# A hybrid attention and retention block in fp32: order of the Strassen sets, of their sums and of their loads

## The chip, the cores and the metric

The kernel runs on one core of a Trainium2 chip. The metric is the device time of one execution in microseconds, as the median of several runs. TensorE (PE) multiplies, VectorE (DVE), ScalarE (ACT) and GpSimd (POOL) do the rest, SyncE (SP) and ACT issue the DMA transfers. Each engine works through its own list of instructions in program order.

## The reference

A layer over 2048 latent tokens and 256 context tokens of width 1024. The input projection makes queries, keys, values and gates for two groups of heads: neighbourhood attention (NA) and retention (RET).

```python
def _mixer(h_lat, h_ctx, w_in, ...):
    na_q, na_k, na_v, na_g, r_q, r_k, r_v, r_g = _split_proj(h_lat @ w_in)   # 8 groups of 512 columns
    cna_q, cna_k, cna_v, cna_g, cr_q, cr_k, cr_v, cr_g = _split_proj(h_ctx @ w_in)
    ...
    y_na = _merge(o_na) * jax.nn.silu(na_g)
    ...
    y_ret = _head_rmsnorm(o_ret, ret_norm_g).astype(dt) * jax.nn.silu(r_g)
    y_lat = jnp.concatenate([y_na, y_ret], axis=-1) @ w_out
```

The change touches the projection of the latent tokens to NA values (columns 1024 to 1535), NA queries (0 to 511), NA gates (1536 to 2047) and RET gates (3584 to 4095).

## The kernel before

Every fp32 operand is cut into a high and a low part (hi and lo, type fp32r); a product is three matmuls: hi by hi, hi by lo, lo by hi. The normalised tokens stand in blocks of 512 tokens, each an hhi and an hlo tile of 128 x 8 x 512 (`blk[b]`); two blocks fit, the others are stored to HBM (hS) and read again. Weights come in halves of 512 KB into st tiles (`load_w`, L176 on SP; four such tiles, each free again when its cuts have read it).

After the keys and the context the program makes two rounds. Round 1 has blocks 0 and 1, round 2 blocks 3 and 2.

1. **Values** (`values`): eight units `u_v`, four with the weights of columns 1024 (two pairs of token groups for each block) and four with those of 1280. A unit is 48 matmuls (L365); ACT evicts one half (L403), VectorE the difference (L404), SP stores it (vB, L413). Between the units' matmuls `h_sums` puts sums of the blocks: two `first`, two `second`, two `third` steps on 128 x 1024 and four `fourth` steps on 128 x 512, each a chain of VectorE adds, an ACT copy (L524) and a subtraction for the low part (L525, on POOL, for one key on VectorE). After units 4 to 6 comes `w_sums` for the first set: p0 cuts a11 and a12, p1 makes four sums and cuts a22, p2 cuts s4, p3 (after unit 7) cuts s3 and s2. Each cut is an ACT copy (L579) and a POOL subtraction (L580).
2. **Six sets** (`strassen`, `w_set`), one for each group of 256 columns in the order of `SETS`: a Strassen scheme with seven products of twelve matmuls (L626). Their order is a11, a12, s4, a22, s2, s3, s1. The function `step(n)` runs after the second, fourth, sixth and seventh product; there the next set's weight sums, the next load_w and the round's other work (`hooks`) are put. Columns under 512 are q: they are scaled, split (L635 ACT, L636 DVE) and stored in 512 KB (qS). The others are gates: Silu (L640) and a store of 256 KB (gS, ggS). `defer` issues a store some ticks later.

The hooks of round 1 store blocks (spill_step), add up the gate of the residual (`wo_gate`, gacc and wraw) and, in the last set, read block 3 and then block 2 (`take`, L769). `wo_open` closes the context's pool, opens the pool gp and clears gacc (L686). Before round 2 the weights of columns 1280 are cut (L336 on ACT, L338 on POOL for the first half and on VectorE for the second). The hooks of round 2 scale the rows of w_out (`wo_mul`, L707 to L712) and store them (woS). After round 2 come the remaining projections (their evictions are at L440), the attention and the output.

Of the kernel before, what the change touches and what calls it, by code (L numbers as in the profile page):

```python
# [9 lines left out]
F32 = mybir.dt.float32  # L10
# [3 lines left out]
ALU = mybir.AluOpType  # L14
# [4 lines left out]
P = 128  # L19
# [63 lines left out]
def hybrid_kernel(ctx: ExitStack, tc: tile.TileContext, a: dict, out: bass.AP):  # L83
    nc = tc.nc
    f = lambda ap: ap[:].bitcast(F32)
# [382 lines left out]

    run_acts(-1)

    SETS = (1536, 1792, 3584, 3840, 0, 256)
    fseq = [(u_rv, 3072), (u_rk, 2560), (u_rq, 2048), (u_rv, 3328), (u_rk, 2816), (u_rq, 2304)]
    fseq += [(u_rv, 3328), (u_rv, 3072), (u_rk, 2560), (u_rq, 2048)]
    CTXU = [(2560, u_rk), (2816, u_rk), (3328, u_rv), (3072, u_rv)]
# [37 lines left out]

    def h_sums(T, A, B):
        (ah, al), (bh, bl) = ((f(x) for x in blk[b]) for b in (A, B))
        tl = {}

        def tile_(key, name, dt=F32R):
            tl[key] = hy.tile([P, 2, KH, 512], dt, name=name)

        V, G = nc.vector.tensor_tensor, nc.gpsimd.tensor_tensor  # L520

        def cut(key, ks, d):
            t = tl[key]
            nc.scalar.copy(t[:, 0, ks, :], d)  # L524
            (V if key == 3 else G)(t[:, 1, ks, :], d, f(t)[:, 0, ks, :], ALU.subtract)  # L525

        def first(c):
            if c == 0:
                tile_(0, "hhi", F32)
                tile_(3, "hlo")  # L530
            ks, kt = slice(2 * c, 2 * c + 2), slice(KH + 2 * c, KH + 2 * c + 2)
            d, e = tl[0][:, 0, ks, :], tl[0][:, 1, ks, :]
            V(d, bh[:, kt, :], bh[:, ks, :], ALU.subtract)
            G(e, bl[:, kt, :], bl[:, ks, :], ALU.subtract)
            V(d, d, e, ALU.add)
            cut(3, ks, d)

        def second(c):
            if c == 0:
                tile_(2, "hhi")  # L540
            ks = slice(2 * c, 2 * c + 2)
            d = tl[0][:, 0, ks, :]
            V(d, d, ah[:, ks, :], ALU.add)
            V(d, d, al[:, ks, :], ALU.add)
            cut(2, ks, d)

        def third(c):
            if c == 0:
                tile_(4, "hlo")
            ks, kt = slice(2 * c, 2 * c + 2), slice(KH + 2 * c, KH + 2 * c + 2)  # L550
            d = tl[0][:, 0, ks, :]
            V(d, ah[:, kt, :], d, ALU.subtract)
            V(d, d, al[:, kt, :], ALU.add)
            cut(4, ks, d)

        def fourth(k):
            if k == 0:
                tile_(1, "hhi")
                T.extend(tl[n] for n in (1, 3, 2, 4))
                tl["o"] = env["st"].tile([P, 2, 512], F32, name="o3", bufs=1)  # L560
            d = tl["o"][:, k % 2, :]
            V(d, bh[:, k, :], ah[:, k, :], ALU.subtract)
            V(d, d, bl[:, k, :], ALU.add)
            V(d, d, al[:, k, :], ALU.subtract)
            cut(1, k, d)

        return [lambda fn=fn, c=c: fn(c) for fn, n in ((first, 2), (second, 2), (third, 2), (fourth, KH)) for c in range(n)]

    def w_sums(rw):
        cut2 = lambda t: t.rearrange("p k w -> p (k w)").rearrange("p (s h k c) -> p s h k c", s=2, h=2, k=KH)  # L570
        a11, a21 = rw[0][:, :, 0:P], rw[0][:, :, P:WG]
        a12, a22 = rw[1][:, :, 0:P], rw[1][:, :, P:WG]
        W, tl = {}, {}

        def cut(key, n, s, r):
            if n not in tl:
                tl[n] = cut2(wa.tile([P, KC, WG], F32R, name=("whi", "wlo")[n % 2]))
            t = W[key] = tl[n][:, s]
            nc.scalar.copy(t[:, 0], r)  # L579
            nc.gpsimd.tensor_tensor(t[:, 1], r, f(t)[:, 0], ALU.subtract)  # L580

        V = nc.vector.tensor_tensor

        def p0():
            cut("a11", 0, 0, a11)
            cut("a12", 0, 1, a12)

        def p1():
            V(a11, a11, a21, ALU.subtract)
            V(a12, a12, a22, ALU.subtract)  # L590
            V(a12, a12, a11, ALU.add)
            V(a21, a21, a22, ALU.add)
            cut("a22", 1, 1, a22)

        def p2():
            cut("s4", 1, 0, a12)
            V(a22, a22, a11, ALU.subtract)

        def p3():
            cut("s3", 2, 1, a11)  # L600
            cut("s2", 2, 0, a22)

        def p4():
            cut("s1", 3, 0, a21)

        return W, [p0, p1, p2, p3, p4, load_w]

    def plain_next(res):
        def p1():
            res.append(w_split(wcur.pop(0), lo=1))  # L610

        return [None, p1, None, None, None, None]

    def w_set(c0, W, T, A, B, mine, ahead, hooks):
        isq = c0 < 512
        t1, t3, t2, t4 = (tuple(t[:, e] for e in range(2)) for t in T)
        b11, b21 = (tuple(x[:, e * KH:(e + 1) * KH, :] for x in blk[A]) for e in range(2))
        b22 = tuple(x[:, KH:, :] for x in blk[B])
        lay = (lambda x: x.rearrange("p (j r c) -> p j r c", r=8, j=4)) if isq else (lambda x: x)
        pv_ = (lambda x: x.rearrange("p (r j c) -> p j r c", r=8, j=4)) if isq else (lambda x: x)  # L620

        def prod(w, h):
            pm = ptile()
            for k in range(KH):
                for i, (ww, hh) in enumerate(((w[:, 0], h[0]), (w[:, 0], h[1]), (w[:, 1], h[0]))):
                    nc.tensor.matmul(pm, ww[:, k, :], hh[:, k, :], start=(k == 0 and i == 0), stop=(k == KH - 1 and i == 2))  # L626
            return pv_(pm)

        def out_tile(extra=False):
            o = env["st"].tile([P, 2, 512], F32R, name="o3", bufs=1) if extra else op.tile([P, 2, 512], F32R, name="o")  # L630
            return o, lay(f(o)[:, 1, :])

        def fin(o, ct, b):
            if isq:
                nc.scalar.activation(o[:, 0, :], f(o)[:, 1, :], AF.Copy, scale=0.125)  # L635
                nc.vector.scalar_tensor_tensor(o[:, 1, :], f(o)[:, 1, :], 0.125, f(o)[:, 0, :], ALU.mult, ALU.subtract)  # L636
                store(qS[c0 // P + ct][b], f(o))
                return
            g = f(o)[:, 1, :]
            nc.scalar.activation(g, g, AF.Silu)  # L640
            dst = gS[(c0 - 1536) // P + ct] if c0 < 2048 else ggS[(c0 - 3584) // P + ct]
            store(dst[:, b * 512:(b + 1) * 512], g)

        def step(n):
            tick()
            for fn in mine[4 + n:5 + n] + ahead[n:n + 1]:
                if fn:
                    fn()
            if hooks:
                for h in hooks.pop(0):  # L650
                    h()

        V = nc.vector.tensor_tensor
        et = wo["p"].tile([P, 2, 512], F32, name="e")
        s1, u3 = (lay(et[:, e, :]) for e in range(2))
        oa, xa = out_tile()
        nc.scalar.copy(s1, prod(W["a11"], b11))
        V(xa, prod(W["a12"], b21), s1, ALU.add)
        step(0)
        m3 = prod(W["s4"], b22)  # L660
        fin(oa, 0, A)
        m4 = prod(W["a22"], t4)
        step(1)
        ob, xb = out_tile(True)
        V(xb, prod(W["s2"], t2), s1, ALU.add)
        V(u3, prod(W["s3"], t3), xb, ALU.add)
        oc, xc = out_tile()
        V(xc, m4, u3, ALU.add)
        V(xb, m3, xb, ALU.add)
        fin(oc, 1, A)  # L670
        step(2)
        m5 = prod(W["s1"], t1)
        od, xd = out_tile()
        V(xb, m5, xb, ALU.add)
        V(xd, m5, u3, ALU.add)
        fin(ob, 0, B)
        fin(od, 1, B)
        step(3)

    wo = {}  # L680
# [51 lines left out]
    def values(ws, bb, hs, hook):  # L732
        vu = [(w, c0, tp) for w, c0 in zip(ws, (1024, 1280)) for b in bb for tp in (2 * b, 2 * b + 1)]
        y = 0
        for n, (w, c0, tp) in enumerate(vu):
            for _ in u_v(w, c0, tp):
                y += 1
                if hs and y % 5 == 0:
                    hs.pop(0)()
            tick()  # L740
            if n == 4:
                W, mine = w_sums(wcur.pop(0))
            if n > 3 and n < 7:
                mine[n - 4]()
            if n in hook:
                hook[n]()
        while hs:
            hs.pop(0)()
        mine[3]()
        return W, mine  # L750
# [10 lines left out]
    for w, c0 in ((w0, 1024), (w1, 1280)):  # L761
        unit(u_v(w, c0, 8))
    T = []
    W, mine = values((w0, w1), (0, 1), h_sums(T, 0, 1), {})
    wo_open()

    def take(b):
        for d in reload_parts(b):
# [2 lines left out]
    hooks = [[spill_step] if n < 16 else [] for n in range(24)]  # L771
# [774 lines left out]
```

## Time and profile before

| what | value |
|---|---|
| median of 3 runs | 1392.61 us (1390.95 to 1395.65) |
| the profiled execution | 1392.92 us, its span 1391.1 us |
| mean granted TensorE clock | 0.984 of full speed |
| busy: PE, DVE, ACT, POOL | 1323.0, 840.3, 591.0, 627.1 us |
| DMA | 295.64 MB, mean 213 GB/s |

The span runs from the first to the last instruction; the profiled execution is 1.8 us longer. Times in rows are from the span's start. Round 1 stands from about 199 to 369 us, round 2 from there to about 569 us. In rows of a timeline the first number is the start, the second the duration, and the bracket at the end is the idle time of the engine before the instruction and what ended it.

### The profile page before, as it was taken

To read this page: it belongs to the slowest core of one execution; us is meant where nothing else is said; L and a number is where in the kernel's file an instruction comes from. 1 tells how busy PE (TensorE), PEld (TensorE's weight loads), DVE (VectorE), ACT (ScalarE), POOL (GpSimd) and SP (SyncE) were. 2 spreads that over 40 slices of the span, in tenths; PEclk is the share of its full clock that TensorE was granted. 3 is DMA by queue.
4 is the path that set the end of the run, shared out by engine and by line. 5 is a ranking of instruction groups with operands and counts; after the bars stand their busy time and mean duration, and the time that the engine had idled before them with its cause. 6 is when DMAs were issued, how large, how long until landed. Compare 5 with 4: busy or idle time off the path is not lost.

```text
span 1391.1 us, 23111 instructions
## 1 busy us (share of the span) xinstructions
PE 1323.0 (95%) x8236; PEld 1157.6 (83%) x8236; DVE 840.3 (60%) x1434; ACT 591.0 (42%) x1239; POOL 627.1 (45%) x585
## 2 busy tenths in 40 slices
PE   6989999899998999899999999999999899999997
PEld 2477999688886777898899899889999789888886
DVE  5787247565676465377766777776663634344445
ACT  4454332333323334265555545456652234433332
POOL 4452434445426556255445434465433145454342
PEclk9999999999989999999999999999999999999999
DMA  9547864596975657976686899967627888555533
GB/s 310 176 166 273 287 193 111 150 351 215 349 222 145 210 189 248 297 200 185 171 225 176 214 262 271 258 181 207 174 87 249 261 289 276 184 169 167 159 114 129
DMA packets 231765, 295.64 MB, mean 213 GB/s; under 512 B 17633, under 2 KB 172385, under 8 KB 230626
## 3 DMA queue, kind: packets, MB, share of 16 engines
q1 hardware_dynamic: 200322, 237.79, 57.9%
q10 hardware_dynamic: 31328, 56.37, 11.3%
q8 instruction: 66, 1.08, 0.3%
q14 instruction: 49, 0.40, 0.1%
HBM read 196.57 MB, written 97.52 MB: 211 GB/s over the span
## 4 chain that ended last, share of the span: by engine, by line
PE 46%; DVE 4%; DMA 2%; ACT 2%; issue 1%; POOL 1%; SPq 0%; ACTq 0%; POOLq 0%; DVEq 0%
PE mm L1390 11%; PE mm L365 10%; PE sS L950 5%; PE mm L354 4%; PE tr L977 3%; PE po L998 3%; PE tr L979 2%; PE mm L1113 2%; PE po L1000 2%; DMA v<-rvS 1%; PE mm L1302 1%; PE mm L1301 1%; PE mm L1300 1%; PE mm L1281 1%; DVE xt L1358 1%
## 5 line engine op out<-in xcount | busy, mean ns | idle before, releaser
L365 PE MATMUL mm<-whi,hhi 128*128 128x256 f32 x768 | 227.1, 296 | 6.3 <-ACT o L440 5.8
L365 PE MATMUL mm<-whi,hlo 128*128 128x256 f32 x768 | 219.6, 286 | 3.3 <-DMA hlo<-hS 3.3
L365 PE MATMUL mm<-wlo,hhi 128*128 128x256 f32 x768 | 219.0, 285 | 0.0
L981 ACT CAST pt<-tr 128x640 fp32r<-128x640 f32 (+1 forms) x128 | 95.6, 747 | 169.6 <-PE tr L979 168.3
L987 DVE TENSOR_TENSOR pt<-tr,pt 128x640 fp32r<-128x640 f32 (+1 forms) x128 | 113.9, 890 | 76.9 <-ACT pt L981 75.6
L365 PEld LDWEIGHTS mm<-whi,hhi 128*128 128x128 f32 x768 | 148.6, 194 | 7.1 <-ACT o L440 6.0
L970 POOL TENSOR_SCALAR sp<-sp,stt 128x640 f32<-128x640 f32 (+2 forms) x128 | 103.0, 807 | 112.8 <-DVE stt L969 71.8
L365 PEld LDWEIGHTS mm<-whi,hlo 128*128 128x128 f32 x768 | 148.9, 194 | 4.4 <-DMA hlo<-hS 4.3
L365 PEld LDWEIGHTS mm<-wlo,hhi 128*128 128x128 f32 x768 | 148.4, 193 | 0.0
L959 DVE CUSTOM_DVE_ANT_0 sp<-sS,nb 128x640 f32<-128x640 f32 (+2 forms) x128 | 105.5, 824 | 29.3 <-PE sS L950 22.3
L964 ACT ACTIVATE sp<-sp,stt 128x640 f32<-128x640 f32 (+2 forms) x128 | 107.4, 839 | 18.9 <-DVE stt L959 17.8
L338 POOL TENSOR_TENSOR wlo<-st,whi 128x256 fp32r<-128x256 f32 (+1 forms) x79 | 83.7, 1073 | 68.8 <-ACT whi L336 67.1
L354 PE MATMUL mm<-hhi,whi 128*128 128x512 f32 x256 | 107.6, 420 | 0.0
L354 PE MATMUL mm<-hlo,whi 128*128 128x512 f32 x256 | 101.8, 398 | 5.4 <-DVE hlo L271 2.3
L950 PE MATMUL sS<-k,q 128*128 128x256 f32 (+3 forms) x512 | 98.8, 315 | 5.2 <-DVE stt L959 4.9
L354 PE MATMUL mm<-hhi,wlo 128*128 128x512 f32 x256 | 101.8, 398 | 0.2 <-DVE wlo L338 0.2
L626 PE MATMUL mm<-hhi,whi 128*128 128x512 f32 x336 | 98.4, 395 | 1.2 <-POOL whi L580 1.0
L1390 PE MATMUL mm<-wor,y 128*128 128x512 f32 x384 | 95.6, 398 | 1.0 <-DVE xt L1399 1.0
L1399 DVE TENSOR_TENSOR xt<-mm,xt 128x512 f32<-128x512 f32 x64 | 43.8, 686 | 86.1 <-PE mm L1390 86.1
L950 PEld LDWEIGHTS sS<-k,q 128*128 128x128 f32 x512 | 82.9, 188 | 11.6 <-DVE stt L959 7.7
L1390 PE MATMUL mm<-won,y 128*128 128x512 f32 x336 | 89.9, 406 | 0.0
L1390 PEld LDWEIGHTS mm<-wor,y 128*128 128x128 f32 x384 | 69.9, 188 | 17.1 <-issue 3.5
(254 smaller groups left out, 3098.3 us busy)
## 6 DMA issues: line engine op xcount, KB each, us to landing
st<-in_w_in_dram SPq DMA_DIRECT2D x64, 512.0 KB
q<-qS SPq DMA_DIRECT2D x64, 256.0 KB
k<-kS SPq DMA_DIRECT2D x16, 576.0 KB
kS<-o SPq DMA_DIRECT2D x16, 512.0 KB
hS<-hhi SPq DMA_DIRECT2D x16, 512.0 KB
hS<-hlo SPq DMA_DIRECT2D x16, 512.0 KB
vB<-o SPq DMA_DIRECT2D x64, 128.0 KB
qS<-o ACTq DMA_DIRECT2D x16, 512.0 KB
```

The source lines that it names most:

```text
L338: eng.tensor_tensor(l, r, f(h), ALU.subtract)
L354: nc.tensor.matmul(pm[:, :n], ww[:, k, cs], h[:, k, :], start=(k == 0 and i == 0), stop=(k == KC - 1 and i == 2))
L365: nc.tensor.matmul(pm[:, t * WG:(t + 1) * WG], h[:, k, o:o + P], ww[:, k, :], start=(k == 0 and i == 0), stop=(k == KC - 1 and i == 2))
L626: nc.tensor.matmul(pm, ww[:, k, :], hh[:, k, :], start=(k == 0 and i == 0), stop=(k == KH - 1 and i == 2))
L950: nc.tensor.matmul(o, hd["q"][i][:, hl, j * P:(j + 1) * P], k, start=(hl == 0), stop=(hl == 1))
L959: nc.vector.tensor_tensor_reduce(T["sp"][:, :n], T["s"], nbz[big][:, o:o + n], -1.0, 3e38, ALU.add, ALU.min, T["st"][:, 0:1])
L964: nc.scalar.activation(sp[:, :n], sp[:, :n], AF.Exp, bias=st[:, 0:1], scale=-1.0, accum_out=st[:, 1:2])
L970: nc.gpsimd.tensor_scalar(sp[:, :n], sp[:, :n], st[:, 2:3], 0.0, ALU.mult, ALU.add)
L981: nc.scalar.copy(pt[:, :ng_ + 2, 0, :], tr[:, :ng_ + 2, :])
L987: nc.vector.tensor_tensor(pt[:, :n, 1, :], tr[:, :n, :], f(pt)[:, :n, 0, :], ALU.subtract)
L1390: nc.tensor.matmul(pm, yy[:, k, :], ww[:, k, sl], start=(k == 0 and i == 0), stop=(k == 3 and i == 2))
L1399: nc.vector.tensor_tensor(xts[t][:, sl], pm, xts[t][:, sl], ALU.add)
```

## The change

1. `SETS` becomes (0, 256, 1536, 1792, 3584, 3840): q sets first, gates last, in both rounds.
2. A gate set puts its fourth result into the free half of the tile of its third (`od` is `oc`), one tile fewer.
3. p0, p1 and p2 of the first set's weight sums come after units 3, 4 and 5 instead of 4, 5 and 6.
4. In `fourth`, the difference of the low parts goes to POOL (e, L563), and VectorE has two operations instead of three.
5. load_w moves from `step(1)` to `step(2)` of each set. In the last set of round 1 that puts it behind the request of block 2.
6. `wo_open` stands before the values of round 1 instead of behind them, since e lives in its pool.
7. The hooks are run in one list with the other steps, in the same order.

```diff
-    SETS = (1536, 1792, 3584, 3840, 0, 256)
+    SETS = (0, 256, 1536, 1792, 3584, 3840)
...
             if k == 0:
                 tile_(1, "hhi")
                 T.extend(tl[n] for n in (1, 3, 2, 4))
-                tl["o"] = env["st"].tile([P, 2, 512], F32, name="o3", bufs=1)
-            d = tl["o"][:, k % 2, :]
+                tl["d"] = env["st"].tile([P, 2, 512], F32, name="o3", bufs=1)
+                tl["e"] = wo["p"].tile([P, 2, 512], F32, name="e")
+            d, e = tl["d"][:, k % 2, :], tl["e"][:, k % 2, :]
+            G(e, bl[:, k, :], al[:, k, :], ALU.subtract)
             V(d, bh[:, k, :], ah[:, k, :], ALU.subtract)
-            V(d, d, bl[:, k, :], ALU.add)
-            V(d, d, al[:, k, :], ALU.subtract)
+            V(d, d, e, ALU.add)
             cut(1, k, d)
...
-        return W, [p0, p1, p2, p3, p4, load_w]
+        return W, [p0, p1, p2, p3, p4, None, load_w]
...
-        return [None, p1, None, None, None, None]
+        return [None, p1, None, None]
...
-        def fin(o, ct, b):
+        def fin(o, ct, b, half=1):
...
-            g = f(o)[:, 1, :]
+            g = f(o)[:, half, :]
...
-            for fn in mine[4 + n:5 + n] + ahead[n:n + 1]:
+            for fn in mine[4 + n:5 + n] + ahead[n:n + 1] + (hooks.pop(0) if hooks else []):
                 if fn:
                     fn()
-            if hooks:
-                for h in hooks.pop(0):
-                    h()
...
-        od, xd = out_tile()
+        od, xd = out_tile() if isq else (oc, f(oc)[:, 0, :])
...
-        fin(od, 1, B)
+        fin(od, 1, B, int(isq))
...
-            if n == 4:
+            if n == 3:
                 W, mine = w_sums(wcur.pop(0))
-            if n > 3 and n < 7:
-                mine[n - 4]()
+            if 3 <= n < 6:
+                mine[n - 3]()
...
+    wo_open()
     W, mine = values((w0, w1), (0, 1), h_sums(T, 0, 1), {})
-    wo_open()
```

In the changed kernel the lines from about L660 on are two lower: L579 and L580 become L580 and L581, L626 becomes L627, L635 and L636 become L636 and L637, L640 becomes L641, L686 becomes L684, L769 becomes L767.

SP at the turn from round 1 to round 2, before: behind the row of wraw come the two halves of the weights of columns 1280, then block 2 (hS_0_91 and hS_1_92), then four halves for the first two sets.

```order
L692 DMA wraw<-in_w_ada_dram 128x1024
L176 DMA st<-in_w_in_dram 128x4x256 x2
L769 DMA hhi<-hS_0_91 128x1024
L769 DMA hlo<-hS_1_92 128x1024
...
L769 DMA hlo<-hS_1_92 128x1024
L176 DMA st<-in_w_in_dram 128x4x256 x4
L413 DMA vB_67<-o 32x2x512 x2
```

The same place now:

```order
L690 DMA wraw<-in_w_ada_dram 128x1024
L767 DMA hhi<-hS_0_91 128x1024
L767 DMA hlo<-hS_1_92 128x1024
...
L767 DMA hlo<-hS_1_92 128x1024
L176 DMA st<-in_w_in_dram 128x4x256 x6
L413 DMA vB_67<-o 32x2x512 x2
```

The two halves have moved behind the eight pieces of block 2, and all six halves stand in one row.

POOL in the values of round 2, before, from the third steps of `h_sums` on (L525) to the first set's cuts of a11 and a12, a22, s4, and s3 and s2 (L580, in this order):

```order
L525 TENSOR_TENSOR hlo<-hhi,hlo 128x1024 x2
L525 TENSOR_TENSOR hhi<-o_3382,hhi 128x512 x2
L580 TENSOR_TENSOR whi<-st,whi 128x512 x2
L525 TENSOR_TENSOR hhi<-o_3382,hhi 128x512
L580 TENSOR_TENSOR wlo<-st,wlo 128x512
L525 TENSOR_TENSOR hhi<-o_3382,hhi 128x512
L580 TENSOR_TENSOR wlo<-st,wlo 128x512
L580 TENSOR_TENSOR whi<-st,whi 128x512 x2
```

The same place now (L563 is e, L581 the old L580):

```order
L525 TENSOR_TENSOR hlo<-hhi,hlo 128x1024 x2
L581 TENSOR_TENSOR whi<-st,whi 128x512 x2
L563 TENSOR_TENSOR e<-hlo 128x512
L525 TENSOR_TENSOR hhi<-o_3384,hhi 128x512
L563 TENSOR_TENSOR e<-hlo 128x512
L525 TENSOR_TENSOR hhi<-o_3384,hhi 128x512
L581 TENSOR_TENSOR wlo<-st,wlo 128x512
L563 TENSOR_TENSOR e<-hlo 128x512
L525 TENSOR_TENSOR hhi<-o_3384,hhi 128x512
L581 TENSOR_TENSOR wlo<-st,wlo 128x512
L563 TENSOR_TENSOR e<-hlo 128x512
L525 TENSOR_TENSOR hhi<-o_3384,hhi 128x512
```

The cuts of a11 and a12 stand ahead of all four fourth steps, a22 ahead of the third and s4 ahead of the last; each fourth step brings an e of its own.

## The prediction

> **What bounds the kernel now.** I read the engine line first, then what TensorE waits for in the stretch the change touches, then the granted clock there, and last the queues behind the two longest waits.
>
> ```profile
> PE 1323.0 (95%) x8236; PEld 1157.6 (83%) x8236; DVE 840.3 (60%) x1434; ACT 591.0 (42%) x1239; POOL 627.1 (45%) x585
> ...
> PE mm L626 <- ACT wlo L579: 8.4, 3, 4.8
> PE mm L365 <- ACT o L440: 5.8, 1, 5.8
> PE mm L626 <- POOL wlo L580: 4.3, 6, 1.3
> PE mm L365 <- DMA hlo<-hS: 3.3, 4, 0.9
> ```
>
> TensorE is busy 95% of the span, and no instruction of it is removed, so the change can only move its waits and its clock. The rows behind the first are the waits between 180 and 580 us (total, times, longest). L626 is a Strassen product that waits for a weight sum; L440 is an eviction behind the end of round 2; the block pieces (hlo from hS) hold the value units of round 2. The windows (length, busy time of PE, PEld, DVE, ACT, POOL, then the granted clock, DMA share, GB/s) show what such a wait costs besides:
>
> ```profile
> 250.00:260.00 10.00, 5.58 (x15) 3.93 (x14) 4.49 (x7) 5.21 (x10) 7.60 (x6) 0.70 0.58 143
> 370.00:385.00 15.00, 12.64 (x98) 12.03 (x98) 9.29 (x6) 3.75 (x5) 9.05 (x3) 0.96 1.04 405
> 380.00:390.00 10.00, 6.19 (x26) 4.72 (x25) 8.30 (x6) 1.88 (x3) 3.14 (x1) 0.68 1.04 395
> 390.00:400.00 10.00, 10.00 (x71) 10.00 (x71) 7.64 (x6) 2.23 (x3) 2.40 (x1) 0.80 0.83 249
> 430.00:440.00 10.00, 4.42 (x12) 2.81 (x11) 6.00 (x9) 5.84 (x12) 5.31 (x5) 0.74 0.59 142
> ```
>
> Around 380 to 400 the waits are short, but the clock falls to 0.68 and 0.80. So block 2 costs TensorE some 3.8 us of waits and, in the 16 us busy there, about 4 us of clock. This looks like the prize of the change. Whether it is depends on what comes last before round 2's sets, so I followed that back:
>
> ```profile
> 435.83 0.80 PE L626 MATMUL mm<-hhi,wlo 128*128 128x512 f32 x1 [4.78 <-ACT wlo L579]
> ...
> 372.91 1.05 ACT L336 CAST whi<-st 128x1024 fp32r<-128x1024 f32 x1 [2.00 <-DMA st<-in_w_in_dram]
> 375.22 1.05 ACT L336 CAST whi<-st 128x1024 fp32r<-128x1024 f32 x1 [1.27 <-DMA st<-in_w_in_dram]
> ...
> 435.16 0.62 ACT L579 CAST wlo<-st 128x512 fp32r<-128x512 f32 x1
> ...
> 376.36 1.23 DVE L338 TENSOR_TENSOR wlo<-st,whi 128x1024 fp32r<-128x1024 f32 x1 [4.72 <-ACT whi L336]
> 377.51 3.42 DVE L533 TENSOR_TENSOR hhi<-hhi 128x1024 f32<-128x1024 f32 x1
> ...
> 413.52 0.69 DVE L404 TENSOR_TENSOR o<-mm,o 128x512 fp32r<-128x512 f32 x1 [1.60 <-ACT o L403]
> ```
>
> TensorE reaches the product with s4 and sits 4.78 us until ACT has cut s4 (435.16). ACT and VectorE come to it at the end of one chain that starts at 377.51 with the first h sum: VectorE adds, ACT cuts, VectorE goes on, with the evictions of the eight value units between. The eviction of unit 3 at 413.52 waited for ACT's half of it (1.60 <-ACT o L403), not for TensorE. Hence in round 2 TensorE runs ahead, and the chain, not the blocks, sets when the product with s4 starts. The chain itself starts with the weights of columns 1280: L336 waits for their second half until 375.22, and L338 and L533 stand behind it.
>
> **The request order.** Here SyncE's rows (start, duration of the group; a second number of some us is time queued):
>
> ```profile
> 360.39 0.33 SPq L692 DMA_DIRECT2D wraw<-in_w_ada_dram  x1
> 362.97 5.35 SPq L176 DMA_DIRECT2D st<-in_w_in_dram  x2
> 368.41 0.46 SPq L769 DMA_DIRECT2D hhi<-hS  x1
> ...
> DMA packets 6710, 15.21 MB, mean 380 GB/s; under 512 B 526, under 2 KB 3598, under 8 KB 6709
> ...
> 389.32 0.58 PE L365 MATMUL mm<-whi,hlo 128*128 128x256 f32 x1 [0.75 <-DMA hlo<-hS]
> ```
>
> The queue is full from 355 to 395, at 405 GB/s in 370 to 385, so a place in it is worth bytes. Block 2 is eight pieces of 512 KB (4.19 MB), the weights two (1.05 MB). With block 2 ahead, the weights land 4.19 MB / 405 GB/s = 10.3 us later: second half at 385.6 instead of 375.2. From the other end: block 2's last piece came at 389.3; without the weights ahead of it, and with 256 KB instead of 512 KB in the four stores of round 1's last set (1.05 MB less), it comes at 389.3 - 5.2 = 384.1, and the two weight pieces at 385.4 and 386.7. If the whole stretch from 358 moves faster for the smaller stores, 384. I take +9.5 us for the start of the chain; the ends are +6 (a part of the pieces of block 2 still behind the weights' packets) and +12. What waits behind it: on ACT, L336 holds the cuts and evictions of units 0 and on; on VectorE, L338 holds L533. TensorE itself has six PSUM tiles for units and goes on to unit 5 before it needs unit 0's; block 2's 3.8 us of waits and its clock go, and are spent waiting for s4. I give them a worth of nothing here; if the chain were not last they would be worth 8.
>
> **Sums a unit sooner, and e on POOL.** These shorten the part of the chain behind unit 3. Durations:
>
> ```profile
> 418.13 0.69 DVE L563 TENSOR_TENSOR o<-o,hlo 128x512 f32<-128x512 f32 x1
> 418.86 1.67 DVE L564 TENSOR_TENSOR o<-o,hlo 128x512 f32<-128x512 f32 x1
> 428.25 0.80 DVE L589 TENSOR_TENSOR st<-st 128x512 f32<-128x512 f32 x1
> 428.97 1.78 DVE L590 TENSOR_TENSOR st<-st 128x512 f32<-128x512 f32 x1
> ...
> 426.50 0.62 ACT L524 CAST hhi<-o 128x512 fp32r<-128x512 f32 x1 [3.80 <-DVE o L564]
> 427.03 0.58 ACT L403 CAST o<-mm 128x512 fp32r<-128x512 f32 x1
> ...
> 413.08 2.40 POOL L525 TENSOR_TENSOR hlo<-hhi,hlo 128x1024 fp32r<-128x1024 f32 x1 [2.24 <-ACT hlo L524]
> 418.28 1.69 POOL L525 TENSOR_TENSOR hhi<-o,hhi 128x512 fp32r<-128x512 f32 x1 [2.80 <-ACT hhi L524]
> 422.50 3.42 POOL L580 TENSOR_TENSOR whi<-st,whi 128x512 fp32r<-128x512 f32 x2
> 427.20 1.29 POOL L525 TENSOR_TENSOR hhi<-o,hhi 128x512 fp32r<-128x512 f32 x1 [1.28 <-ACT hhi L524]
> 436.08 1.72 POOL L580 TENSOR_TENSOR wlo<-st,wlo 128x512 fp32r<-128x512 f32 x1
> ```
>
> I lay the new order on the old times. POOL: L525 to 415.5, the two cuts of a11 and a12 (3.42) to 418.9, e0 (as L525, 1.29) to 420.2. VectorE adds e0 (0.69) to 420.9, ACT cuts (0.62) to 421.5, POOL cuts (1.29) and makes e1 to 424.1; add and cut to 425.4; unit 4's eviction, ACT 0.58 and VectorE 0.69, to 426.7. The four sums of p1 took 3.8 us beside one POOL cut; now they stand beside two and e2, so 4.8, to 431.5. f2's two operations to 432.9, cut and eviction of unit 5 on ACT to 434.1, then s4's high half to 434.7 (was 435.78) and its low half on POOL, behind f2's cut, to 436.3 (was 437.80). That is 1.5 us sooner; the ends are 0 and 3. VectorE loses one operation of 0.69 us for each of four sums, but each now waits for a POOL operation of 1.29. Behind s4, e3 and its cut stand ahead of s3 and s2 on POOL: s2's low half comes some 7 us behind s4's low half instead of 2.5, and TensorE asks for it after the rest of s4 and all of a22, also about 6 to 7 us. I take 0.5 us of new wait (0 to 2).
>
> VectorE's 1.67 instead of 0.69 falls beside a POOL operation (L525 at 418.28 ends at 419.97, and 419.97 plus some 0.6 is where L564 ends). [...]
>
> **Round 1** has the same reorder, and one new piece at its start:
>
> ```profile
> 254.98 0.91 DVE L686 MEMSET gacc<- 128x1024 f32 x1 [0.16 <-issue]
> ...
> 253.38 0.50 PE L626 MATMUL mm<-hhi,wlo 128*128 128x512 f32 x1 [3.13 <-ACT wlo L579]
> 255.40 1.22 PE L626 MATMUL mm<-hhi,wlo 128*128 128x512 f32 x2 [1.29 <-POOL wlo L580]
> ```
>
> Clearing gacc lay in VectorE's free time; now it stands ahead of the first h sum: +0.9. Sooner sums -1.5, wait for s2 +0.5. Its wait for s4, 3.13 + 1.29 us, shrinks to some 3. The clock lost about 2 us here (0.70 over 5.6 busy us, and a little behind); rows say that waits as short as 0.9 us cost clock too (380 to 390), so I take 0.5 of these 2. Round 1: -0.6 us, ends -4 and +1.5.
>
> [...]
>
> **q first, gates last, shared output tile, load one step later.** The adds and stores of the q sets (L635 and L636, 512 KB each) move from the ends of the rounds to their starts, where the queue has room: 143 and 142 GB/s in the windows above. Nothing in those sets is waited for. A set takes some 19.6 us (six of them between 255.40 and the L336 at 372.91), so a product 2.8. A load_w one step later, behind the sixth product instead of the fourth, has the seventh and two of the next set, 8.4 us, until that set's first cut asks for it, and a pair of 512 KB pieces takes 2.6 us at 405 GB/s; I cost it at nothing, and if the queue is full it is a few us of ACT, hidden by a set's lead. At round 2's end:
>
> ```profile
> 568.58 0.62 ACT L709 CAST g<-wraw 128x512 fp32r<-128x512 f32 x1 [6.73 <-DMA woS<-g]
> 569.11 0.62 ACT L635 ACTIVATE o<-o 128x512 fp32r<-128x512 f32 x1
> ...
> 574.10 0.58 ACT L440 COPY o<-mm 128x512 f32<-128x512 f32 x1
> ...
> 574.73 0.58 PE L365 MATMUL mm<-whi,hhi 128*128 128x256 f32 x1 [5.76 <-ACT o L440]
> ```
>
> ACT is late there because the store of woS lands late, behind larger stores. Smaller ones (0.5 to 1 MB less, 1.3 to 2.6 us at 405 GB/s) bring it forward: -2.0, ends -5.8 and +1 (the store is held by SyncE's loads instead).
>
> **Sum.** Round 1 -0.6; start of round 2's chain +9.5, its reorder -1.5, wait for s2 +0.5; end -2.0: +5.9 us. The profiled execution took 1392.92, 0.3 above the median of 1392.61; so 1398.5.
>
> **Rivals.** (1) The weights cost what I say but half as much: they land near 380, or the reorder saves 3 us. Then round 2 loses 4 us instead of 8.5, round 1 and the end give back 2 to 4: 1389 to 1396, about 1394. For it: three terms of mine are rounded against the change. Against: the queue's 405 GB/s leaves no room. (2) Faster: the request order does not hold up the chain. Place: L336 before unit 0's eviction. If its second half starts before 378.5, the chain starts within 3 us of before, and the reorder (-3), round 1 with its clock (-4) and an end without its wait (-5.8) decide: 1392.6 + 3 - 12.8, or 1383 at best, 1387 in the middle. Against: eight requests stand ahead of the weights on the one queue. [...]
>
> **How the numbers follow.** This kernel's runs tell about 0.3% (4.2 us) from no change. Forecast as summed, 1397 to 1402: 0.46. Rival 1: 0.27, nearly all of it within 0.3%. Rival 2: 0.18, nearly all faster. Rival 3: 0.09. Faster 0.19, same 0.28, slower 0.53. The range 1388 to 1404 leaves out the better half of rival 2 and the worst of rival 3.
>
> **What would show it.** Right: L336's second half of the 1280 weights starts at 383 to 387 and L533 behind it; block 2's waits (L365 from hS) gone; TensorE's wait for ACT L580 (the old L579) in round 2 at 11 us or more, over the two waits ahead of it and of the a11 cut; the clock near 1.00 from 380 to 400. Wrong: the second L336 before 379; or TensorE waiting elsewhere in the sets (a later load_w); or the end of round 2 without a wait, which would show as L440 not among TensorE's releasers.

## The result, and the profile after

The changed kernel takes 1416.19 us (median of 4 runs, 1412.18 to 1418.29) against 1393.78 us before: 1.0159 times, 95% interval 1.0129 to 1.0189. It is 22 us slower. The forecast had the direction, but 1398.5 us and a range that ended at 1404.

TensorE's waits between 180 and 620 us (total, times, longest), the changed kernel:

```profile
PE mm L627 <- ACT wlo L580: 12.4, 5, 8.8
PE mm L627 <- ACT whi L580: 10.8, 4, 8.4
PE mm L627 <- POOL whi L581: 7.9, 7, 1.9
PE mm L627 <- POOL wlo L581: 5.3, 8, 1.3
PE mm L365 <- ACT o L440: 3.8, 1, 3.8
PE mm L365 <- DMA hlo<-hS: 0.7, 1, 0.7
```

Block 2's waits have shrunk to 0.7 us. In their place stand 36 us of waits of the Strassen products (L627) for weight sums, against 13.7 before. Where the two longest come from is read off ACT, VectorE and TensorE at the turn between the rounds:

```profile
392.76 1.05 ACT L336 CAST whi<-st 128x1024 fp32r<-128x1024 f32 x1 [14.05 <-DMA st<-in_w_in_dram]
394.18 1.05 ACT L336 CAST whi<-st 128x1024 fp32r<-128x1024 f32 x1 [0.37 <-DMA st<-in_w_in_dram]
...
397.36 3.42 DVE L533 TENSOR_TENSOR hhi<-hhi 128x1024 f32<-128x1024 f32 x1
...
433.87 0.79 PE L627 MATMUL mm<-hhi,whi 128*128 128x512 f32 x1 [8.42 <-ACT whi L580]
...
453.68 0.79 PE L627 MATMUL mm<-hhi,wlo 128*128 128x512 f32 x1 [8.83 <-ACT wlo L580]
```

The weights of columns 1280 came 19 us later than before (394.18 against 375.22), the first h sum of round 2 20 us later (397.36 against 377.51), and TensorE waited 8.4 us for a11 and 8.8 for s4. But only a part of the 19 us is the queue's: the first request of block 3 was already 7.8 us late, at 362.78 where it stood at 354.98 before (the first row is the kernel before, the second the changed one):

```profile
354.98 0.34 SPq L769 DMA_DIRECT2D hhi<-hS  x1
...
362.78 0.34 SPq L767 DMA_DIRECT2D hhi<-hS  x1
```

Some 4 us of the 7.8 stand at the first h sum of round 1 already (203.74 against 199.96): 0.9 are the clearing of gacc, the rest lies ahead of all that was changed and differs from one profiled execution to the next (198.7 to 203.8 in the kernels below). The other 4 were lost in round 1. So round 1 had lost time before the turn, where the forecast had a small gain. Round 1's start in the changed kernel:

```profile
255.00 0.50 PE L627 MATMUL mm<-hhi,wlo 128*128 128x512 f32 x1 [2.06 <-ACT wlo L580]
257.02 0.73 PE L627 MATMUL mm<-hhi,wlo 128*128 128x512 f32 x2 [1.28 <-POOL wlo L581]
263.20 0.74 PE L627 MATMUL mm<-hhi,whi 128*128 128x512 f32 x2 [0.81 <-ACT whi L580]
265.26 4.01 PE L627 MATMUL mm<-hhi,whi 128*128 128x512 f32 x10 [1.33 <-POOL whi L581]
281.17 0.73 PE L627 MATMUL mm<-hhi,wlo 128*128 128x512 f32 x2 [0.33 <-POOL wlo L581]
287.64 0.74 PE L627 MATMUL mm<-hhi,whi 128*128 128x512 f32 x2 [1.10 <-ACT whi L580]
```

The wait for s4 shrank as forecast (3.3 us instead of 4.4), but behind it stand new ones for s2 (263 to 265) and again in the second set (281 to 288).

### The profile page after: what moved, and what is told of

Same layout as the page of the kernel before. It is cut to its first block, busy times and chain, and to the rows that moved or that the text cites. A ratio compares the mean times of both kernels' runs of the same rounds, so it can differ in the third digit from the quotient of the medians.

```text
span 1416.4 us, 23115 instructions
## 1 busy us (share of the span) xinstructions
PE 1329.0 (94%) x8236; PEld 1157.1 (82%) x8236; DVE 834.6 (59%) x1426; ACT 590.2 (42%) x1239; POOL 636.0 (45%) x593
## 4 chain that ended last, share of the span: by engine, by line
PE 60%; DVE 13%; DMA 9%; issue 6%; POOL 5%; ACT 4%; SPq 2%; ACTq 0%; POOLq 0%; DVEq 0%
PE mm L365 12%; PE mm L1388 11%; PE mm L354 8%; PE mm L627 6%; PE sS L948 5%; PE tr L975 3%; PE po L996 3%; PE mm L1111 2%; DMA woS<-g 2%; PE tr L977 2%; PE po L998 2%; PE mm L302 2%; DMA v<-rvS 2%; DMA vB<-o 2%; SPq L413 1%
## 5 line engine op out<-in xcount | busy, mean ns | idle before, releaser
L627 PE MATMUL mm<-hhi,whi 128*128 128x512 f32 x336 | 104.4, 413 | 19.3 <-ACT whi L580 10.8
L354 PE MATMUL mm<-hhi,whi 128*128 128x512 f32 x256 | 108.9, 425 | 0.0
L627 PEld LDWEIGHTS mm<-hhi,whi 128*128 128x128 f32 x336 | 65.5, 198 | 40.3 <-ACT whi L580 13.4
```

The source lines that it names most:

```text
L354: nc.tensor.matmul(pm[:, :n], ww[:, k, cs], h[:, k, :], start=(k == 0 and i == 0), stop=(k == KC - 1 and i == 2))
```

## The experiments

Times are medians, with the difference to the kernel before in the runs of the same chip job, and the interval of the ratio.

**1. load_w back in its old place** (in the changed kernel):

```diff
-        return W, [p0, p1, p2, p3, p4, None, load_w]
+        return W, [p0, p1, p2, p3, p4, load_w]
```

> The changed kernel (1416 us) with load_w back behind the fourth product of each set, so the weights of columns 1280 stand ahead of block 2 again. Theory 1 (the place in the queue costs 10 to 11 us through the chain that starts with the cut of these weights, the q sets at the start of a round cost 6 to 8 in all, the sooner sums give back some 3): second L336 of round 2's start at most 12 us behind the last set's block request of round 1 less than before's 20 us plus 3, 1405 us. Theory 2 (all of the loss is the set order): no change, 1414 to 1418. Theory 3 (e on POOL slows the chain and is the loss): no change either.

1402.78 us, +10.2 (1.0063 to 1.011). The later load costs 12 us (22.4 less 10.2), near the 10 to 11 of theory 1. But 10 us remain, where only the order of the sets should have cost.

**2. The old order of the sets** (in the changed kernel): `SETS = (1536, 1792, 3584, 3840, 0, 256)`.

> The changed kernel with the old order of the sets, gates first and q last, and all else changed. Theory 1: the waits of TensorE for ACT and POOL in the first three sets of each round go, 6 to 8 us less; the larger q stores stand ahead of the weights again, 1 to 2 us more: 1409. Theory 2: 1393 to 1398. Theory 3: 1416.

1407.47 us, +14.9 (1.0103 to 1.0156). The old order gives back 7.5 us, near theory 1, for a reason that the next two take apart.

**3. Both back.** What is left are the sooner sums, e on POOL, the shared tile and the earlier clearing of gacc.

> The changed kernel with both back: old set order and load_w in its old place. What is left of the change is the sums a unit sooner, e on POOL, the shared tile of a gate set and gacc cleared earlier. Theory 1: 1.5 us less at s4 in each round, 0.5 to 2 more at s2, so 1390 to 1394, no difference from before. Theory 3: 1400 or more, with VectorE's L564 and L565 at 1.7 us each and s4 cut later after unit 3's eviction than before's 21.6 us.

1397.70 us, +5.1 (1.0027 to 1.0066). Neither theory: these edits cost, with the gates first too.

**4. q first alone** (in the kernel before): `SETS = (0, 256, 1536, 1792, 3584, 3840)`.

> The kernel before with nothing changed but the order of the sets: q first, gates last. Theory 1: 4 to 8 us more in the first sets of the two rounds, where the sums of the next set stand on ACT behind the work of the q set; 2 less at the end of round 2: 1397 to 1401. Theory 2: 1410 or more. If the set order only hurts together with e on POOL or the shared tile, 1392 to 1394.

1388.10 us, -4.5 (0.9955 to 0.9986). The order of the sets, which theories 1 and 2 blamed, is a gain. Theory 1 falls in this part, and theory 2 altogether. What remains is that the order hurts only together with other edits: with q first, the kernel of 1 is 5.1 us slower than that of 3. From here on the base is this kernel.

**5. e back on VectorE** (in the kernel of 1): the changed kernel with early load_w and with the three old operations of `fourth`.

> The changed kernel with load_w in its old place (1402.8 us) and, besides, all three operations of a fourth h sum back on VectorE. Left of the change: q first, sums a unit sooner, shared tile, gacc cleared earlier. Theory A (e on POOL is what costs: it puts a POOL operation of 1.3 us and a wait of VectorE into every link of the chain, and s3 and s2 come late behind it): 1386 to 1390, as with q first alone (1388.1). Theory B (the sums a unit sooner cost: they stand ahead of evictions and h sums): stays at 1400 or more. Theory C (the shared tile): stays at 1400 or more, with VectorE waiting in the gate sets for stores.

1396.57 us, +3.7 (1.0015 to 1.0044): 6.5 less than with e, but still 8.2 above q first alone. Both A and another cause.

**6. q first and e on POOL** (with gacc cleared earlier).

> The kernel before with q first (1388.1 us) and e on POOL, and gacc cleared earlier, which e needs; sums at their old place, no shared tile, load_w at its old place. Theory A: 1396 to 1403, with VectorE's L565 waiting for POOL. Theories B and C: 1387 to 1390.

1395.81 us, +3.0 (1.0002 to 1.0035): e with gacc costs 7.5 us.

**7. q first and load_w later in every set** (the edit of 1, the other way).

> The kernel before with q first (1388.1 us) and load_w one step later in every set, so that the weights of columns 1280 stand behind block 2. If their place in the queue sets the start of the chain, L533 of round 2 comes 9 to 12 us later, block 2's waits go, TensorE waits 8 us or more for s4 and for a11: 1397 to 1401. If the loss seen between the kernels with and without this edit came from later loads in the other sets, TensorE's new waits stand in the sets and L533 comes no later.

1403.67 us, +10.9 (1.0048 to 1.0092): 15.3 above q first alone, and more than the 1401 expected at most.

**8. q first, block 2 ahead, and the cut of the 1280 weights in the chain:**

```diff
-    hooks[21].insert(0, lambda: take(2))
+    hooks[21] = (lambda: take(2), *hooks[21])      # run ahead of load_w in this step
...
-    w0, w1 = mid + [w_split(wcur.pop(0), lo=1)]
-    load_w()
+    w1, parts = w_parts(wcur.pop(0), 1)            # the parts run after unit 1, then load_w, then wo_gate(7)
     load_w()
```

> The kernel before with q first (1388.1 us), block 2 requested ahead of the weights of columns 1280 in round 1's last set alone, and the cut of these weights (L336, L338) put behind unit 1 of round 2, so that the chain need not wait for them. If the chain's start is what the weights' place costs, L533 starts 3 to 6 us earlier than 377.5 with block 2's waits gone too, TensorE waits less for s4, and the time is 1382 to 1386. If the place costs in another way (units short of weights, fuller queue), it is 1390 or more.

1385.51 us, -7.3 (0.9922 to 0.9961), the fastest here. Its turn, ACT and VectorE:

```profile
386.83 2.00 ACT L336 CAST whi<-st 128x1024 fp32r<-128x1024 f32 x2
...
371.39 2.46 DVE L533 TENSOR_TENSOR hhi<-hhi 128x1024 f32<-128x1024 f32 x1
```

The chain starts at 371.39, 6 us before the kernel before, although the weights are cut only at 386.83. Against q first alone the gain is 2.8 us, about the size of the intervals. The wait for s4 in round 2 was expected to shrink and did not (5.97 us, against 4.78 before and 6.27 with q first alone): the whole round comes sooner.

**9. q first and the sums a unit sooner**, nothing else:

```diff
-            if n == 4:
+            if n == 3:
...
-            if n > 3 and n < 7:
-                mine[n - 4]()
+            if 3 <= n < 6:
+                mine[n - 3]()
```

> The kernel before with q first (1388.1 us) and the sums p0 to p2 a unit sooner, nothing else. The kernel with these two, the shared tile and gacc cleared earlier took 1396.6. If the sums are what costs there (s4 sooner, but a fourth h sum then stands between s4 and s3, so that s3 and s2 come later than TensorE asks for them, and the q set's stores stretch it): 1393 to 1397, with TensorE waiting for POOL or ACT at the fifth product of the first two sets. If the shared tile or the clearing of gacc costs: 1387 to 1390.

1394.26 us, +1.3 (0.9998 to 1.0029): 5.8 above q first alone. The sums cost, not the shared tile. POOL in round 1, first with q first alone, then with the sooner sums (the first L580 with wlo is s4, the row with whi x2 is s3 and s2):

```profile
253.41 1.27 POOL L525 TENSOR_TENSOR hhi<-o,hhi 128x512 fp32r<-128x512 f32 x1 [4.66 <-ACT hhi L524]
254.63 1.72 POOL L580 TENSOR_TENSOR wlo<-st,wlo 128x512 fp32r<-128x512 f32 x1
256.31 2.52 POOL L580 TENSOR_TENSOR whi<-st,whi 128x512 fp32r<-128x512 f32 x2
```

```profile
248.34 1.73 POOL L580 TENSOR_TENSOR wlo<-st,wlo 128x512 fp32r<-128x512 f32 x1
252.80 1.29 POOL L525 TENSOR_TENSOR hhi<-o,hhi 128x512 fp32r<-128x512 f32 x1 [2.73 <-ACT hhi L524]
256.30 2.51 POOL L580 TENSOR_TENSOR whi<-st,whi 128x512 fp32r<-128x512 f32 x2 [2.21 <-ACT whi L579]
```

The chains start at 200.94 and 198.66. So s4 comes 53.7 and 49.7 us behind the start, 4.0 sooner; s3 and s2 come at 55.4 and 57.6, 2.3 later. In round 2 the same: s4 4.0 sooner, s3 and s2 2.8 later.

**10. The fourth h sums behind p3** (in the kernel of 1). Only the seventh product reads them.

```diff
-                if hs and y % 5 == 0:
+                if len(hs) > KH and y % 5 == 0:
...
+        mine[3]()
         while hs:
             hs.pop(0)()
-        mine[3]()
```

> The changed kernel with load_w in its old place (1402.8 us) and all four fourth h sums put behind p3, that is behind the last of the first set's weight sums; only the seventh product of the set reads them. e stays on POOL. If s3 and s2 behind the fourth sums are the loss, s4, s3 and s2 come 8 us or more sooner and the waits at the start of both rounds go: 1380 to 1388. If e on POOL costs by itself (contention with VectorE) or the stores of the q sets do, the fourth sums now delay the evictions of the first set instead: 1395 to 1403.

1409.44 us, +16.5 (1.009 to 1.0135): 6.3 worse instead of 15 or more better. A miss; run 11 shows what comes of such an order.

**11. The same on the kernel of 8**, with the sooner sums and all on VectorE.

> The kernel with q first, block 2 ahead and the 1280 cut in the chain (1385.5 us), and besides the sums p0 to p2 a unit sooner and the fourth h sums behind p3, all on VectorE. If the first set's waits come from the fourth sums ahead of the weight sums, TensorE's waits for s4 (3.2 + 1.3 us in round 1, 6.0 + 0.8 in round 2) go and the clock after them stays up: 1373 to 1378. If the seventh product or the first set's evictions then wait for the fourth sums, 1382 to 1386.

1390.69 us, -2.3 (0.9975 to 1.0004): 5.0 worse than the kernel of 8. TensorE at the start of round 1:

```profile
264.11 2.61 PE L626 MATMUL mm<-hhi,wlo 128*128 128x512 f32 x10 [0.86 <-POOL wlo L580]
271.33 0.47 PE L626 MATMUL mm<-hhi,whi 128*128 128x512 f32 x1 [1.87 <-DVE o L663]
275.18 0.50 PE L626 MATMUL mm<-hhi,wlo 128*128 128x512 f32 x1 [0.87 <-ACT wlo L579]
277.07 1.15 PE L626 MATMUL mm<-hhi,wlo 128*128 128x512 f32 x2 [1.16 <-POOL wlo L580]
```

The waits for the first set's s4 are gone; the last product (264), VectorE's sums of results (271) and the next set's sums (275 to 277) are late instead. The chain does not end with the first set: what is pushed behind one sum comes out at the next.

**12. Block 2 ahead in that one queue alone:** the first half of the edit of 8, without the second.

> The kernel before with q first (1388.1 us) and block 2 ahead of the weights of columns 1280 in round 1's last set alone; load_w in all other sets at its old place, the cut of these weights at its old place too. With load_w late in every set the time was 1403.7. If the place in that one queue is all of it: L533 of round 2 some 13 us later than with q first alone, 1400 to 1404. If the later loads of the other sets cost too, 1392 to 1398. The kernel with the same request order and the cut behind unit 1 took 1385.5, so the difference between the two is what the chain's start is worth.

1403.31 us, +11.5 (1.0054 to 1.0108), the same as with load_w late in every set. So all of edit 5's cost is the turn, and the kernels of 8 and 12, with the same request order of block 2 and these weights, differ by 18 to 19 us. (Behind unit 1 the kernel of 8 also has one later load of weights.) ACT and TensorE in the kernel of 12:

```profile
386.69 1.05 ACT L336 CAST whi<-st 128x1024 fp32r<-128x1024 f32 x1 [0.38 <-DMA st<-in_w_in_dram]
...
434.43 0.80 PE L626 MATMUL mm<-hhi,whi 128*128 128x512 f32 x1 [16.47 <-ACT whi L579]
...
447.97 0.79 PE L626 MATMUL mm<-hhi,wlo 128*128 128x512 f32 x1 [4.24 <-ACT wlo L579]
```

**13. q first and gacc cleared earlier.**

> The kernel before with q first (1388.1 us) and gacc cleared before the values of round 1 instead of behind them, nothing else. With e on POOL besides it took 1395.8. If the clearing alone stands in VectorE's chain: 0.9 us later, 1388 to 1390, and e on POOL costs 6 to 7. If the earlier opening of the pool costs more (its first transfers, or memory that is shared with the context's tiles): 1392 to 1396, and e costs little.

1389.29 us, -2.6 (0.997 to 1.0002): 1.9 above q first alone, with an interval of some 2 us. The rest of the 7.5 of run 6, about 5.6, is e.

## Why the prediction was wrong

The edits, each measured on the kernel with q first, as differences to the kernel before of their own chip job:

| edit | forecast | measured |
|---|---|---|
| q first, gates last | 0 in the sets, -2.0 at the end | -4.5 |
| block 2 ahead of the weights | +9.5 | +15.9 (run 12) |
| load_w late in the other sets | 0 | -0.6 (run 7 less run 12) |
| sums a unit sooner | -1.5 + 0.5 in each round | +5.8 |
| e on POOL | within the row above | +5.6 |
| gacc cleared earlier | +0.9 | +1.9 |
| shared tile | 0 | 0.5 (run 5 less runs 9 and 13) |
| clock in round 1 | -0.5 | in the rows above |
| sum | +5.9 | about +25 (the kernel: +22.4) |

Each measured row has an interval of some 2 to 4 us. With q first as the base the rows add up to the whole within that, so no interplay clear of the noise is shown there. But the order of the sets does not simply add to the others: alone it gains 4.5 us, on top of the sums, e, gacc and the tile it costs 5.1 (run 1 against run 3), and in the whole change 7.5 (against run 2).

**The turn: mechanism right, term too small.** The request order holds up the chain, block 2's own waits are worth nothing while the chain is last (run 12 has only 0.9 us of them left and is slower), and freeing the chain from the weights turns the same order into a gain (run 8). The term was mis-sized: the first h sum of round 2 starts 188.9 us behind that of round 1 in run 12 and 175.3 with q first alone, 13.7 us later, where I had 9.5. The weights land 13.3 us later (second cut at 386.69 against 373.37), and the trace shows where: SyncE sends their request 12.7 us later. First its row with q first alone, then in run 12 the first and the last of block 2's eight requests and the weights:

```profile
364.37 0.93 SPq L176 DMA_DIRECT2D st<-in_w_in_dram  x2
```

```profile
364.58 0.38 SPq L767 DMA_DIRECT2D hhi<-hS  x1
...
376.68 0.32 SPq L767 DMA_DIRECT2D hlo<-hS  x1
377.10 13.22 SPq L176 DMA_DIRECT2D st<-in_w_in_dram  x6
```

SyncE's rows stand in the order of the requests, and between these eight it stands idle for 9.5 us, which ends with landings of gate stores (5.2 us), of pieces of block 3 (3.4) and of wraw (0.9). The forecast priced the bytes of block 2 alone, 10.3 us; by how much the stores in the same stretch make the difference was not tested. Some 2 us more are lost in the sets behind: the window from 450 to 480 us has the clock at 0.93 in run 12, over 30 us busy, and at 1.00 with q first alone and in the kernel before.

```profile
450.00:480.00 30.00, 30.00 (x121) 24.22 (x122) 16.72 (x22) 12.30 (x22) 18.10 (x14) 0.93 0.70 229
```

**The sums: the failing step.** The forecast gave the sooner sums and e -2.0 us over both rounds; measured are +11.4, and these 13.4 us are the larger part of the miss. "That is 1.5 us sooner" was about right for s4 (2.2 in round 1 and 1.7 in round 2 of the kernel of 1; 4.0 without e), but I priced the chain at s4, where TensorE waited, and not at its end. The sentence on s3 and s2 saw s2's low half come "some 7 us behind s4's low half instead of 2.5" and gave it 0.5 us, as if TensorE came to it no sooner. In the changed kernel it ends 8.2 us behind s4's in round 1 (these rows; 9.6 in round 2), and TensorE waits 0.81 and 1.33 us for s3 and s2 (263 to 265 above):

```profile
255.25 1.72 POOL L581 TENSOR_TENSOR wlo<-st,wlo 128x512 fp32r<-128x512 f32 x1
262.71 2.50 POOL L581 TENSOR_TENSOR whi<-st,whi 128x512 fp32r<-128x512 f32 x2 [1.29 <-ACT whi L580]
```

With q first, by the places of s3 and s2 behind the start of the chain, round 1, the costs rise with them: 55.4 us with q first alone, 57.6 with the sums, 56.5 with e, 59.0 with both; round 2: 60.4, 63.1, 63.0 and 65.4 to 66.0. And what s2 costs comes again in the second set, with the clock on top, as these windows from 280 to 300 show, the kernel of 1 first, then q first alone:

```profile
280.00:290.00 10.00, 6.34 (x22) 4.49 (x21) 3.92 (x5) 4.60 (x9) 5.03 (x4) 0.81 0.75 266
290.00:300.00 10.00, 10.00 (x39) 8.00 (x38) 9.29 (x11) 1.00 (x2) 3.34 (x3) 0.85 0.98 315
```

```profile
280.00:290.00 10.00, 10.00 (x44) 8.03 (x44) 7.31 (x7) 2.75 (x6) 7.55 (x6) 1.00 1.01 386
290.00:300.00 10.00, 10.00 (x46) 8.17 (x44) 7.35 (x11) 4.34 (x8) 2.46 (x2) 1.00 0.99 362
```

In the kernel of 1 there stands a wait that the forecast did not have either. VectorE's last sum of the first q set waits for a tile whose store has not landed, ACT's scaling waits for it, and the cut of the second set's s3 and s2 behind that:

```profile
281.74 0.69 DVE L673 TENSOR_TENSOR o<-mm,e 128x512 f32<-128x512 f32 x1 [4.55 <-DMA qS<-o]
...
282.46 0.63 ACT L636 ACTIVATE o<-o 128x512 fp32r<-128x512 f32 x1 [4.56 <-DVE o L673]
283.06 1.12 ACTq L150 DMA_DIRECT2D qS<-o  x2
284.27 1.14 ACT L580 CAST whi<-st 128x512 fp32r<-128x512 f32 x2 [1.18 <-DVE o L637]
```

With q first alone that wait is 1.6 us and no wait of TensorE follows it. "Nothing in those sets is waited for" thus holds only while the chain is early enough. With the gates first (run 3), s3 and s2 come nearly as late (57.9 us behind the start of the chain in round 1, 59.0 in the kernel of 1), but TensorE has no wait between 262 and 300 and keeps its clock:

```profile
280.00:290.00 10.00, 10.00 (x45) 8.02 (x44) 9.07 (x10) 1.42 (x3) 2.85 (x2) 1.00 1.05 372
290.00:300.00 10.00, 10.00 (x45) 8.23 (x44) 4.40 (x5) 5.50 (x10) 8.03 (x6) 1.00 0.84 311
```

So the same edits cost 5.1 us there and 14.7 with q first (run 1 against run 4). Which part of this is the store's was not tested: no run gives the q sets a further tile.

**e on POOL: rival 3 in size only.** Its 0.09 and the 1404 at the end of the range stand on an estimate of mine, up to 3 us a round from VectorE's operations growing longer beside POOL's (1.67 us instead of 0.69 in the kernel before). No run shows that loss; e costs 2.8 us a round in another way. In round 1 of run 6 one sum of p1 (L592) takes 1.63 us instead of 0.69, beside an e of 1.71 us on POOL. The additions of e keep 0.69 us; three of the four wait 2.72 to 3.69 us for e, which stands on POOL behind the cut of the sum before (VectorE in run 6):

```profile
235.40 0.69 DVE L565 TENSOR_TENSOR o<-o,e 128x512 f32<-128x512 f32 x1 [3.55 <-POOL e L563]
239.41 0.69 DVE L565 TENSOR_TENSOR o<-o,e 128x512 f32<-128x512 f32 x1 [2.72 <-POOL e L563]
246.37 0.69 DVE L565 TENSOR_TENSOR o<-o,e 128x512 f32<-128x512 f32 x1 [3.69 <-POOL e L563]
```

One operation of 0.69 us was saved, and a loop through POOL, VectorE, ACT and POOL again was closed around each of the four sums.

**q first** gains more than the 2.0 I gave it at the end: the weights of columns 1280 land earlier too (the second half's cut at 172.4 us behind the first h sum instead of 175.3). The last set before the turn now stores 256 KB pieces; that this is the reason was not tested. The end of round 2 waits 3.75 us in the changed kernel instead of 5.76 (3.92 with q first alone), the 2.0 forecast.

**The other steps.** Round 1 "-0.6" was the sum of the wrong terms. Clearing gacc stands in the trace with its 0.91 us; the +1.9 of run 13 has an interval of some 2. The clock of round 1's start did rise in the changed kernel, as forecast (0.97 instead of 0.94 over 240 to 300 us). What the forecast did not have is the clock in round 2 behind the longer waits of 8.4 and 8.8 us. Over 420 to 480 us, first the kernel before, then the changed one:

```profile
420.00:480.00 60.00, 54.08 (x235) 42.87 (x234) 36.72 (x46) 23.42 (x42) 35.74 (x26) 0.94 0.60 175
```

```profile
420.00:480.00 60.00, 38.31 (x143) 28.65 (x142) 37.73 (x40) 18.40 (x31) 34.77 (x23) 0.77 0.51 131
```

By the busy time, that is some 9 us of clock instead of 3. It spends what came back in block 2's stretch, where the clock is 1.00 instead of 0.90 (369 to 420 us).

## What to carry to other kernels

Where several engines pass one chain along, price an edit at the last link that anyone waits for, not at the link where the wait stands now: the wait moves to whatever the edit pushed back (run 9: s4 4.0 us sooner, s3 and s2 2.3 later in round 1, 5.8 us slower). When two transfers compete for a full queue, ask which one stands at the head of a chain; if the urgent one can't go first, move its consumer out of the chain's way (run 8), which here was worth 18 to 19 us. An operation given to another engine is no saving when its result must come back within the same link (e on POOL: 5.6 us slower). And an order that gains by itself can cost on top of another edit (q first: -4.5 us alone, +5.1 in run 1 against run 3): try it both ways.

## What the runs showed of the hardware

The kernel before has a clock of 0.68 from 380 to 390, where no wait of TensorE is longer than 0.91 us, and still 0.80 from 390 to 400, where it is busy throughout. With two waits of 2.33 and 1.33 us (kernel of 1, 285 to 288) the windows from 280 to 300 have 0.81 and 0.85, against 1.00 with q first alone, without the waits. Waits of 1.10 and 1.33 us at the same place in the changed kernel (288 to 290) left the clock at 1.00 in both windows. How much waiting it takes is not worked out by any run here.
